# Multiplying the conditioning vector into two weight blocks on TensorE instead of VectorE

## The chip, the cores and the metric

The kernel runs on one core of one Trainium2 chip, one launch for the whole layer. Its engines are named as in the profile: PE is TensorE's matmuls, PEld its weight loads, DVE is VectorE, ACT is ScalarE, POOL is GpSimd, SP is the engine that issues most loads. The metric is the device time of one launch in microseconds, as the median of several runs.

## The reference, cut to what matters

The layer is a decoder block of 1024 tokens and 1024 channels, all in 32-bit floats. A vector `c` conditions it: six vectors of 1024 (shift, scale and gate of two sub-layers) come from one product with a 1024 x 6144 matrix.

```python
c_act = jax.nn.silu(c)
ada = c_act @ ada_w[l] + ada_b[l]
sh1, sc1, gt1, sh2, sc2, gt2 = jnp.split(ada, 6, axis=-1)
h = rmsnorm(x, norm1_g[l]) * (1.0 + sc1) + sh1
z = h @ w_in[l]
q_lat, kv_lat, k_rope, conv_in, gate_logits = jnp.split(z, SPLIT_POINTS, axis=-1)
...
u = glu_a * jax.nn.sigmoid(glu_b)          # the halves of conv_in
u = causal_depthwise_conv(u, conv_w[l], conv_b[l])      # 31 taps, 512 channels
u = jax.nn.silu(layernorm(u, conv_ln_g[l], conv_ln_b[l]))
```

After that come latent attention, the merge of both branches by gates, and a mixture of 32 experts. The change touches the two vectors `sh1` and `sc1` alone, which every column of `h` needs before the first product with `w_in`, and one place in the gates.

## The kernel before, in words

The sums are kept exact by splitting each operand of a large product into a high and a low part (`w_split`, `lo_part`: ACT casts the high part, POOL or DVE subtracts it from the whole). Each product of 128 x 512 is then three PE matmuls.

**The front.** Tokens come in two halves of four tiles, `x0` to `x3` and `x4` to `x7`. A tile is squared with its sum on ACT (`x_square`), its inverse root is found on DVE in Newton steps (`rsqrt_steps`), it is scaled (`x_scales`: tile 6 on ACT, tile 3 on POOL, the others on DVE) and transposed on PE (`x_trans2`, `x_trans`), so that channels lie on partitions: eight blocks `k` of 128 channels for each half. A block is then modulated by its 128 columns of scale and shift (`modulate`), split into high and low (`hi` on ACT, `lo`), and multiplied with the first two pairs of columns of the convolution's input, `wa0`, `wb0`, `wa1`, `wb1` (`prod_h`, `prod_l`, called by `prods`): 12 matmuls for a block and both pairs.

**The modulation.** The first two blocks of `ada_w` (8 MB) are loaded in five steps, for channel blocks 0, 1, (2, 3), (4, 5) and (6, 7). With the matrix's 1024 rows as eight on each partition, `ada_init` and `ada_products` multiply each of the eight slices by its column of `c` and add them up in two accumulators, one DVE instruction for a slice (`ad` times `cact` onto `ac`; the first two slices of steps 3 and 4 are on ACT), and a last instruction adds the two. `ada_sum` sums over partitions on PE, with a column of ones as the moving operand; `modulation` adds the bias. This work is woven between the Newton steps of the next tiles (`weave`, `halves`).

**What sets the order.** In the front the order on PE, ACT, POOL and SP is the order in which the code is written (`manual_schedule`), and the same holds on DVE until the last `u` of the first half, `glu(1, 0, ...)`. After that DVE's order is the scheduler's: the rotary tables, the masks of positions, then the convolution's taps (`conv_taps`, line 757) between the products of `glu` (`u`, line 546). The next blocks of `ada_w` are accumulated between the taps (`ada_block`, line 479).

SP's queue issues the loads in the order in which they are wanted: `x0` to `x3`, step 0 of `ada_w`, the first halves of `wa0` and `wb0`, and so on, up to steps 3 and 4 with `x4` to `x7` behind them. A load waits where its buffer isn't free: two quarters of step 3 take the buffers of `wa0` and `wb0`, and so wait for the subtraction of their second halves on POOL (line 501).

**The convolution's statistics.** The gates are 16 columns `m`, each 48 matmuls on PE (`pg`). After column 5 `conv_stats` transposes the convolution's result on PE (`cT`, line 834) and takes each token's mean and variance on DVE. Its sums are `cacc`, one tile of 128 channels each, four in all; each is done when DVE has put 31 taps on it.

Of the kernel before, what the change touches and what calls it, by code (L numbers as in the profile page):

```python
# [14 lines left out]
F32 = mybir.dt.float32  # L15
# [36 lines left out]
def hybrid_layer(ctx: ExitStack, tc: tile.TileContext, x, c, positions, ada_w, ada_b, norm1_g,  # L52
# [76 lines left out]
    def run(steps):  # L129
        for _ in steps:  # L130
            pass
# [27 lines left out]
    # constants  # L159
# [24 lines left out]
    # vectors that are wanted as columns: one stack of rows, one transpose  # L184
# [27 lines left out]
    # rotary tables, [token, tile, frequency]  # L212
# [65 lines left out]
    cact = consts.tile([P, KD], F32, name="cact")  # L278

    def silu_c():  # L280
        cs_t = pro.tile([P, KD], F32, name="cs_t")
        A.activation(cs_t, c_sb, AF.Tanh, scale=0.5)
        V.scalar_tensor_tensor(cact, cs_t, 1.0, c_sb, op0=OP.add, op1=OP.mult)
        V.tensor_scalar_mul(cact, cact, 0.5)

    # positions: mask of the diagonal blocks, and whether the tiles follow one another
# [61 lines left out]
    XE, SUM, HN = 2, (1, 1, 2), ((2, 2), (0, 2), (0, 2))  # L348
    B0, W0, B1, B2, B3, W4, MB, LO = 4, 2, 2, 2, 6, 2, V, G
    XA, XP = (6,), (3,)  # L350
    ADD, TR, G0, CC0 = 1, (1, 2, 3), 0, 7
# [61 lines left out]
    def ada_init(j, eng):  # L413
        wd = len(STEPS[j]) * P
        g = D // (2 * wd)
        ada_acc[j] = [sa.tile([P, 2, wd], F32, name=f"ac{j}{i}", tag="th" if i else "gt", bufs=2) for i in range(2)]
        for k in range(2):
            a, w, c1 = ada_acc[j][k], adaw_[j][k // g][:, k % g], cact[:, k:k + 1]
            if eng is A:
                A.activation(a.rearrange("p a b -> p (a b)"), w.rearrange("p a b -> p (a b)"), AF.Copy, scale=c1)  # L420
            else:
                V.tensor_scalar(a, w, c1, 0.0, op0=OP.mult, op1=OP.add)
                yield

    def ada_products(j):
        g = D // (2 * len(STEPS[j]) * P)
        acc = ada_acc[j]
        for k in range(2, KD):
            V.scalar_tensor_tensor(acc[k % 2], adaw_[j][k // g][:, k % g], cact[:, k:k + 1], acc[k % 2],
                                   op0=OP.mult, op1=OP.add)  # L430
            yield
        if ADD:
            V.tensor_tensor(acc[0], acc[0], acc[1], op=OP.add)
            yield

    def ada_sum(j):
        ada_ps[j] = ps_o(f"pf{j}")
        m = len(STEPS[j])
        for i in range(2 * m):
            b, jj = divmod(i, m)  # L440
            for h in range(2 - ADD):
                PE.matmul(ada_ps[j][:, i:i + 1], ada_acc[j][h][:, b, jj * P:(jj + 1) * P], ones_c,
                          start=h == 0, stop=h == 1 - ADD)
# [24 lines left out]
    AB, AR, HS, CM = 9, 12, 2, 6  # L468
# [93 lines left out]
    # loads, in the order in which they are wanted  # L562
# [51 lines left out]
    def some(g, n):  # L614
        for _ in range(n):
            next(g, None)
# [14 lines left out]

    run(x_norm(0, 2))
    x23 = x_norm(2, 4)
    some(x23, B0)
    run(ada_init(0, V))
    weave(x23, ada_products(0), W0)
# [3 lines left out]
    column_vectors(0, R_N2)  # L640
    x_trans2(0, 2)
    ada_sum(0)
    run(modulation(0))
    p1 = itertools.chain(ada_init(1, V), ada_products(1))
    some(p1, B1)
    modulate(0, V)
    hi(0, 0)
    x_trans2(2, 2)
    some(p1, 2)
    lo(0, 0, V)  # L650
    prod_h((0,), 0, 0)
    split_part(w1, 0)
    prod_l((0,), 0, 0)
    run(p1)
    p2 = itertools.chain(ada_init(2, V), ada_products(2))
    some(p2, B2)
    x_trans2(4, 2)
    ada_sum(1)
    x_trans2(6, 2)
    run(modulation(1))  # L660
    modulate(1, V)
    hi(0, 1)
    lo(0, 1)
    split_part(w0, 1)
    split_part(w1, 1)
    prods((1,), 0, (0,))
    run(p2)
    run(ada_init(3, A))
    prods((0, 1), 0, (1,), SUM[0], 2)

    def halves(s, later, n0, n1):
        ka, kb = STEPS[s]
        some(later, n0)
        run(modulation(s))
        modulate(ka, V)
        hi(0, ka)
        modulate(kb, MB)
        hi(0, kb)
        some(later, n1)
        lo(0, ka)  # L680
        lo(0, kb, LO)
        run(later)

    halves(2, ada_products(3), *HN[0])
    prods((0, 1), 0, STEPS[2], SUM[1], 3)
    for t in range(4, 4 + XE):
        x_square(t)
    run(ada_init(4, A))
    xe = x_norm(4, 4 + XE)
    some(xe, B3)  # L690
    p4 = weaved(ada_products(4), xe, W4)
    halves(3, p4, *HN[1])
    prods((0, 1), 0, STEPS[3], SUM[2], 4)
    for t in range(4 + XE, NT):
        x_square(t)
    halves(4, x_norm(4 + XE, 8), *HN[2])
# [171 lines left out]
    for m in range(16):  # L868
# [6 lines left out]
        if m == 5:  # L875
            tokn = conv_stats()
# [67 lines left out]
    # q weights with the norm's gain: per head [nope | pe | pe turned], the other way round for odd heads  # L944
# [33 lines left out]
    # tables that the transposed queries are multiplied by  # L978
# [121 lines left out]
    # keys: the first half twice, so that the next pair's can be made ahead  # L1100
# [35 lines left out]
    # tiles of queries, two heads at a time: scores run ahead of the transposed probabilities, these of the values  # L1136
# [78 lines left out]
    # any order of positions: every block of keys, masks from the positions  # L1215
# [66 lines left out]
    # the router's weights with the second norm's scale, its shift as a constant row  # L1282
# [114 lines left out]
    def keep_warm(n_, tag, b_):  # L1397
        # products of no use: without work for some microseconds the tensor engine's clock would be halved
# [35 lines left out]
    # a weight tile takes over the slot of one that is used shortly before it is wanted: gathers go first  # L1434
# [22 lines left out]
    # experts by turns from the groups  # L1457
# [73 lines left out]
    # the order of the products, and after how many more of them each later step of a tile is issued  # L1531
# [53 lines left out]
    # the experts after the first EARLY: sorted by their numbers of rows, those of groups 0, 2 and of 1, 3 by turns;  # L1585
    # place by place fewer rows are provided for
# [129 lines left out]
    # the rows of the last experts are added on chip: to each token its row, by a product with a 0-1 matrix  # L1716
# [18 lines left out]
    for i in range(E + AHEAD[-1]):  # L1735
# [13 lines left out]
        if i == JOIN:  # L1749
            with tc.issue_after(split_[PB]):  # L1750
# [8 lines left out]
                # rows beyond those provided for: counted from 128  # L1759
# [178 lines left out]
```

## Time and profile before

| | |
|---|---|
| median of 3 runs | 1101.34 us (1100.28 to 1103.8) |
| the profiled execution | span 1093.9 us from the first to the last instruction; its time around the span is not listed apart |
| PE busy | 995.7 us, 91% of the span |
| DVE busy | 796.1 us, 73% |
| ACT, POOL busy | 437.3 us, 422.0 us |
| granted TensorE clock, mean | 0.953 |

The shares are means over stages with different limits. In the first 330 us or so DVE is busy almost all the time, and PE stops now and then; later PE is busy without a break for long stretches, and DVE is not. The span is 7.4 us below the median of the runs; a difference within the span is taken as a difference of the time.

### The profile page before, as it was taken

The numbers are of one execution on the slowest core, as the hardware profiler recorded it, in microseconds if no ns is written. First come the engines' busy times: TensorE is split into PE (matmuls) and PEld (weight loads), VectorE is DVE, ScalarE is ACT, GpSimd is POOL, SyncE is SP. The second block draws the span as 40 slices with busy tenths as digits, with TensorE's granted clock in tenths as the row PEclk, the third lists the DMA queues.
The fourth block names the chain that finished last, engine by engine and source line by source line (L and its number), as shares of the span: only waits on it lengthen the run. The fifth ranks groups of instructions, "written<-read, shape, count | busy, mean of one in ns | idle before, by whom it ended". The sixth has DMA issues, their size and how long they took to land. (4 is left out here: it accounts for less than half of the span.)

```text
span 1093.9 us, 16693 instructions
## 1 busy us (share of the span) xinstructions
PE 995.7 (91%) x5744; PEld 841.5 (77%) x5744; DVE 796.1 (73%) x1839; ACT 437.3 (40%) x914; POOL 422.0 (39%) x361
## 2 busy tenths in 40 slices
PE   4697979999599999999999998899998999999991
PEld 2576869988477788778888877678886999997881
DVE  7989999999989815547556665964447888875555
ACT  4453312212123334347666773232223555543343
POOL 5555929823121114114333446630004464454111
PEclk9798989999899999999999999999999999997876
DMA  9902521246574263710000016684656989998813
GB/s 305 307 8 58 140 70 37 92 159 183 172 228 140 105 213 130 249 41 1 1 2 17 6 59 200 212 300 163 258 189 240 314 284 282 301 272 227 269 77 155
DMA packets 97743, 176.79 MB, mean 162 GB/s; under 512 B 14123, under 2 KB 53116, under 8 KB 97648
## 3 DMA queue, kind: packets, MB, share of 16 engines
q1 hardware_dynamic: 82736, 148.33, 40.8%
q0 software_dynamic: 9152, 16.28, 6.3%
q10 hardware_dynamic: 5760, 11.01, 2.8%
q8 instruction: 48, 0.79, 0.3%
q14 instruction: 47, 0.39, 0.1%
HBM read 145.22 MB, written 40.35 MB: 170 GB/s over the span
## 5 line engine op out<-in xcount | busy, mean ns | idle before, releaser
L757 DVE SCALAR_TENSOR_TENSOR cacc<-u,cw,cacc 128x1024 f32<-128x1024 f32 x120 | 173.2, 1496 | 0.0
L1676 PE MATMUL pe<-xT,rg 128*128 128x128 f32 (+7 forms) x512 | 78.9, 288 | 0.1
L1676 PEld LDWEIGHTS pe<-xT,rg 128*128 128x128 f32 x512 | 73.2, 204 | 5.6 <-ACT xT L1671 0.5
L1671 ACT ACTIVATE xT<-xp,h2c 128x128 f32<-128x128 f32 (+7 forms) x128 | 52.4, 434 | 53.4 <-DVE xT L1668 28.8
L1676 PE MATMUL pe<-xT,ru 128*128 128x128 f32 (+7 forms) x512 | 68.8, 293 | 0.0
L1676 PEld LDWEIGHTS pe<-xT,ru 128*128 128x128 f32 x512 | 66.0, 209 | 0.0
L1705 POOL DMA_INDIRECT yscr<-ob,srci x18 | 33.6, 1868 | 59.4 <-DVE ob L1699 30.4
L105 PE MATMUL po<-woh,y 128*128 128x512 f32 x128 | 53.7, 419 | 1.4 <-DVE gm L1331 1.4
L1668 DVE TENSOR_SCALAR xT<-xp,h2c 128x128 f32<-128x128 f32 (+7 forms) x128 | 45.4, 381 | 10.3 <-ACT xT L1671 9.9
L107 PE MATMUL po<-woh,y 128*128 128x512 f32 x128 | 50.4, 394 | 0.0
L106 PE MATMUL po<-wol,y 128*128 128x512 f32 x128 | 50.3, 393 | 0.0
L873 ACT ACTIVATE gt<-pg 128x512 f32<-128x512 f32 x32 | 19.0, 594 | 68.9 <-PE pg L107 68.9
L1518 POOL TENSOR_SCALAR x1n<-x,rst 128x1024 f32<-128x1024 f32 x8 | 9.0, 1121 | 93.9 <-DVE rst L127 82.4
L479 DVE SCALAR_TENSOR_TENSOR acc<-aw,cact,acc 128x1024 f32<-128x1024 f32 x28 | 39.8, 1421 | 3.2 <-DMA aw<-in_ada_w_dram 3.2
L1663 PE MATMUL xp<-ident,xg 128*128 128x128 f32 (+7 forms) x256 | 39.0, 276 | 1.8 <-DMA xg<-xscr,si 1.8
L1655 DVE TENSOR_TENSOR rdl<-rd,rdh 128x1024 fp32r<-128x1024 f32 x30 | 36.7, 1223 | 5.3 <-ACT rdh L1654 5.2
L1654 ACT CAST rdh<-rd 128x1024 fp32r<-128x1024 f32 x30 | 31.4, 1045 | 18.9 <-PE pd L107 17.8
L1081 PE MATMUL mo<-pT,V 128*64 128x128 f32 x576 | 38.5, 278 | 0.0
L1699 DVE SCALAR_TENSOR_TENSOR ob<-pd,wvp,gt2b 128x512 f32<-128x512 f32 (+7 forms) x36 | 26.4, 744 | 16.6 <-DMA yscr<-ob,srci 12.5
L1663 PEld LDWEIGHTS xp<-ident,xg 128*128 128x128 f32 (+7 forms) x256 | 33.5, 194 | 4.0 <-DVE eid L1619 2.6
L1332 POOL TENSOR_TENSOR gm<-gm 128x512 f32<-128x512 f32 x16 | 27.5, 1726 | 22.0 <-DVE gm L1331 19.4
L1081 PEld LDWEIGHTS mo<-pT,V 128*64 128x64 f32 x576 | 30.8, 136 | 5.7 <-issue 5.7
(2071 smaller groups left out, 3141.2 us busy)
## 6 DMA issues: line engine op xcount, KB each, us to landing
aw<-in_ada_w_dram SPq DMA_DIRECT2D x32, 512.0 KB, 3.8
rg<-in_expert_w_gate_dram SPq DMA_DIRECT2D x32, 512.0 KB, 9.6
ru<-in_expert_w_up_dram SPq DMA_DIRECT2D x32, 512.0 KB, 9.2
rd<-in_expert_w_down_dram SPq DMA_DIRECT2D x32, 512.0 KB, 9.3
x<-in_x_dram SPq DMA_DIRECT2D x16, 512.0 KB, 5.5
ad<-in_ada_w_dram SPq DMA_DIRECT2D x32, 256.0 KB, 5.5
wg<-in_w_in_dram SPq DMA_DIRECT2D x16, 512.0 KB, 4.9
gscr<-gt ACTq DMA_DIRECT2D x32, 256.0 KB, 2.9
```

What stands on the lines that cost most here:

```text
L105: PE.matmul(ps, lh, rh, start=first, stop=False)
L106: PE.matmul(ps, lh, rl, start=False, stop=False)
L107: PE.matmul(ps, ll, rh, start=False, stop=last)
L479: V.scalar_tensor_tensor(acc, w, cact[:, k:k + 1], acc, op0=OP.mult, op1=OP.add)
L757: V.scalar_tensor_tensor(a, u[j][:, k:k + T], cw[:, j, k:k + 1], a, op0=OP.mult, op1=OP.add)
L1081: PE.matmul(po[par * DV:(par + 1) * DV, i % 4 * P:(i % 4 + 1) * P], Vt[b][:, 2 * pr + par], pTs[par][:, b * P:(b + 1) * P], start=(b == 0) ...
L1655: V.tensor_tensor(rdl, rd, f32(rdh), op=OP.subtract)
L1663: PE.transpose(p[:, c], xv[:, k, :], ident[:m, :m])
L1668: split_.append(V.tensor_scalar(xT[:, ks], p[:, c], h2c[:, 0, k:k + 1], h2c[:, 1, k:k + 1], op0=OP.mult, op1=OP.add).ins)
L1671: A.activation(xT[:, ks], p[:, c], AF.Identity, scale=h2c[:, 0, k:k + 1], bias=h2c[:, 1, k:k + 1])
L1676: PE.matmul(pa[:, o:o + m], w[:, k * P:(k + 1) * P], xT[:, k * P:k * P + m], start=(k == 0), stop=(k == KD - 1))
L1705: s_ = G.indirect_dma_start(out=yscr, out_offset=bass.IndirectOffsetOnAxis(ap=src[:m], axis=0), in_=ob[:m], in_offset=None, bounds_check=T ...
```

## The change

The eight products of a step are done on PE now (`ada_mm`). `silu_c` writes `c` 32 times side by side (`crep`), so that a slice's column of `c` is a stationary operand of 128 rows and 32 columns, and the slice of `ada_w` is the moving operand, 256 or 512 columns wide. Slices 0 to 3 go to four different groups of 32 partitions of one PSUM bank, slices 4 to 7 are added to them. ACT copies the bank to `ac`, and `ada_sum` sums over the four groups with a column that is one at partitions 0, 32, 64 and 96 (`sel4`). Nothing of a step is left on DVE but `modulation` and `modulate`; the low parts of the first half's blocks are all subtracted on DVE now, of which seven were on POOL. The Newton steps of the tiles are no longer woven with anything, and those of tiles 6 and 7, with their squares, stand behind step 4's split. `conv_stats` is called after gate column 6, `conv_act` and the later blocks of `ada_w` one or two columns later.

```diff
     cact = consts.tile([P, KD], F32, name="cact")
+    crep_ = []
+    sel4 = pro.tile([P, 1], F32, name="sel4")
 
     def silu_c():
         cs_t = pro.tile([P, KD], F32, name="cs_t")
         A.activation(cs_t, c_sb, AF.Tanh, scale=0.5)
         V.scalar_tensor_tensor(cact, cs_t, 1.0, c_sb, op0=OP.add, op1=OP.mult)
         V.tensor_scalar_mul(cact, cact, 0.5)
...
+        crep = sa.tile([P, KD, 32], F32, name="crep", tag="gt", bufs=2)
+        crep_.append(crep)
+        V.tensor_copy(crep, cact[:, :, None].to_broadcast([P, KD, 32]))
+
+        si = pro.tile([P, 1], I32, name="sel4i")
+        V.tensor_single_scalar(si, pidx_i, 31, op=OP.bitwise_and)
+        V.tensor_scalar(sel4, si, 0.0, None, op0=OP.is_equal)
...
-    XE, SUM, HN = 2, (1, 1, 2), ((2, 2), (0, 2), (0, 2))
-    B0, W0, B1, B2, B3, W4, MB, LO = 4, 2, 2, 2, 6, 2, V, G
+    XE, SUM = 2, (1, 2, 4)
     XA, XP = (6,), (3,)
-    ADD, TR, G0, CC0 = 1, (1, 2, 3), 0, 7
+    TR, G0, CC0 = (1, 2, 3), 0, 7
...
-    def ada_init(j, eng):
+    def ada_mm(j):
+
         wd = len(STEPS[j]) * P
         g = D // (2 * wd)
-        ada_acc[j] = [sa.tile([P, 2, wd], F32, name=f"ac{j}{i}", tag="th" if i else "gt", bufs=2) for i in range(2)]
-        for k in range(2):
-            a, w, c1 = ada_acc[j][k], adaw_[j][k // g][:, k % g], cact[:, k:k + 1]
-            if eng is A:
-                A.activation(a.rearrange("p a b -> p (a b)"), w.rearrange("p a b -> p (a b)"), AF.Copy, scale=c1)
-            else:
-                V.tensor_scalar(a, w, c1, 0.0, op0=OP.mult, op1=OP.add)
-                yield
-
-    def ada_products(j):
-        g = D // (2 * len(STEPS[j]) * P)
-        acc = ada_acc[j]
-        for k in range(2, KD):
-            V.scalar_tensor_tensor(acc[k % 2], adaw_[j][k // g][:, k % g], cact[:, k:k + 1], acc[k % 2],
-                                   op0=OP.mult, op1=OP.add)
-            yield
-        if ADD:
-            V.tensor_tensor(acc[0], acc[0], acc[1], op=OP.add)
-            yield
+        p = ps_o(f"am{j}")
+        for k in range(KD):
+            q = 32 * (k % 4)
+            PE.matmul(p[q:q + 32, :2 * wd], crep_[0][:, k], adaw_[j][k // g][:, k % g].rearrange("p b n -> p (b n)"),
+                      start=k < 4, stop=k >= 4)
+        ada_acc[j] = sa.tile([P, 2, wd], F32, name=f"ac{j}", tag="th", bufs=2)
+        A.copy(ada_acc[j].rearrange("p b n -> p (b n)"), p[:, :2 * wd])
 
     def ada_sum(j):
         ada_ps[j] = ps_o(f"pf{j}")
         m = len(STEPS[j])
         for i in range(2 * m):
             b, jj = divmod(i, m)
-            for h in range(2 - ADD):
-                PE.matmul(ada_ps[j][:, i:i + 1], ada_acc[j][h][:, b, jj * P:(jj + 1) * P], ones_c,
-                          start=h == 0, stop=h == 1 - ADD)
+            PE.matmul(ada_ps[j][:, i:i + 1], ada_acc[j][:, b, jj * P:(jj + 1) * P], sel4, start=True, stop=True)
 
...
-    AB, AR, HS, CM = 9, 12, 2, 6
+    AB, AR, HS, CM = 10, 14, 2, 8
...
+    def step(j, eng):
+        run(modulation(j))
+        for k in STEPS[j]:
+            modulate(k, V)
+        for k in STEPS[j]:
+            hi(0, k)
+            lo(0, k, eng)
+
     run(x_norm(0, 2))
-    x23 = x_norm(2, 4)
-    some(x23, B0)
-    run(ada_init(0, V))
-    weave(x23, ada_products(0), W0)
+    run(x_norm(2, 4))
     for k in range(0, KD, 2):
         x_trans2(k, 0)
     split_part(w0, 0)
     column_vectors(0, R_N2)
+    ada_mm(0)
     x_trans2(0, 2)
+    x_trans2(2, 2)
     ada_sum(0)
-    run(modulation(0))
-    p1 = itertools.chain(ada_init(1, V), ada_products(1))
-    some(p1, B1)
-    modulate(0, V)
-    hi(0, 0)
-    x_trans2(2, 2)
-    some(p1, 2)
-    lo(0, 0, V)
+    step(0, V)
+    x_trans2(4, 2)
+    ada_mm(1)
+    x_trans2(6, 2)
+    split_part(w1, 0)
     prod_h((0,), 0, 0)
-    split_part(w1, 0)
+    ada_sum(1)
+    step(1, V)
     prod_l((0,), 0, 0)
-    run(p1)
-    p2 = itertools.chain(ada_init(2, V), ada_products(2))
-    some(p2, B2)
-    x_trans2(4, 2)
-    ada_sum(1)
-    x_trans2(6, 2)
-    run(modulation(1))
-    modulate(1, V)
-    hi(0, 1)
-    lo(0, 1)
+    prods((1,), 0, (0,))
     split_part(w0, 1)
     split_part(w1, 1)
-    prods((1,), 0, (0,))
-    run(p2)
-    run(ada_init(3, A))
+    ada_mm(2)
     prods((0, 1), 0, (1,), SUM[0], 2)
-
-    def halves(s, later, n0, n1):
-        ka, kb = STEPS[s]
-        some(later, n0)
-        run(modulation(s))
-        modulate(ka, V)
-        hi(0, ka)
-        modulate(kb, MB)
-        hi(0, kb)
-        some(later, n1)
-        lo(0, ka)
-        lo(0, kb, LO)
-        run(later)
-
-    halves(2, ada_products(3), *HN[0])
-    prods((0, 1), 0, STEPS[2], SUM[1], 3)
+    step(2, V)
+    ada_mm(3)
     for t in range(4, 4 + XE):
         x_square(t)
-    run(ada_init(4, A))
-    xe = x_norm(4, 4 + XE)
-    some(xe, B3)
-    p4 = weaved(ada_products(4), xe, W4)
-    halves(3, p4, *HN[1])
+    prods((0, 1), 0, STEPS[2], SUM[1], 3)
+    step(3, V)
+    run(x_norm(4, 4 + XE))
+    ada_mm(4)
     prods((0, 1), 0, STEPS[3], SUM[2], 4)
+    step(4, V)
     for t in range(4 + XE, NT):
         x_square(t)
-    halves(4, x_norm(4 + XE, 8), *HN[2])
+    run(x_norm(4 + XE, 8))
...
-        if m == 5:
+        if m == 6:
             tokn = conv_stats()
         if m in (CM, CM + 1):
             conv_act(m - CM, tokn)
```

On PE, at the end of the front, `am` is the bank that the new products write, `ad` the loaded slices, `pf` the sum over partitions, and `pa`, `pb` the products of the first half. In the changed kernel the stretch around step 4's products reads:

```order
L598 MATMUL pa_262<-hT0l,wa1h 128x512
L598 MATMUL pb_263<-hT0l,wb1h 128x512
L428 MATMUL am_561<-ad_231,crep 32x512 x2
L428 MATMUL am_561<-ad_232,crep 32x512 x2
L428 MATMUL am_561<-ad_233,crep 32x512 x2
L428 MATMUL am_561<-ad_234,crep 32x512 x2
L592 MATMUL pa_260<-hT0h,wa0h 128x512
L593 MATMUL pa_260<-hT0h,wa0l 128x512
```

All 24 products of channel blocks 4 and 5 now stand between these eight and the sum `pf` of step 4; before, 12 of them stood ahead of that sum and 12 behind it.

On ACT, in the same place, `hT0h` is a block's high part, the line with `ms` is a square with its sum, and `th` is the `tanh` of the first `glu`. Before:

```order
L627 CAST hT0h<-xn_346 128x512
L360 ACTIVATE hT1l,ms<-x_242 128x1024
L360 ACTIVATE hT1l,ms<-x_244 128x1024
L627 CAST hT0h<-xn_353 128x512
L627 CAST hT0h<-xn_355 128x512
L367 ACTIVATE x_242<-x_242,rstd 128x1024
L545 ACTIVATE th_681<-pb_255 128x512
```

And now:

```order
L622 CAST hT0h<-xn_341 128x512
L431 COPY ac_570<-am_561 128x512
L622 CAST hT0h<-xn_348 128x512
L622 CAST hT0h<-xn_350 128x512
L368 ACTIVATE hT1l,ms<-x_243 128x1024
L368 ACTIVATE hT1l,ms<-x_245 128x1024
L375 ACTIVATE x_243<-x_243,rstd 128x1024
L540 ACTIVATE th_687<-pb_261 128x512
```

The squares of tiles 6 and 7 moved from ahead of the last two blocks' high parts to behind them, next to the scaling of tile 6 that needs their result.

On PE, at the statistics, `pg` is a gate product and the four tiles `cacc` are told apart by their numbers. Before:

```order
L834 MATMUL cT_2302<-ident,cacc_1189 128x128
L834 MATMUL cT_2302<-ident,cacc_1221 128x128
L834 MATMUL cT_2310<-ident,cacc_1189 128x128
L834 MATMUL cT_2310<-ident,cacc_1221 128x128
L105 MATMUL pg_2452<-hT0h,wg6h 128x512
L106 MATMUL pg_2452<-hT0l,wg6h 128x512
L107 MATMUL pg_2452<-hT0h,wg6l 128x512
L834 MATMUL cT_2302<-ident,cacc_1253 128x128
L834 MATMUL cT_2310<-ident,cacc_1253 128x128
```

And now:

```order
L107 MATMUL pg_2334<-hT1h,wg6l 128x512
L809 MATMUL cT_2370<-ident,cacc_1195 128x128
L809 MATMUL cT_2370<-ident,cacc_1227 128x128
L809 MATMUL cT_2370<-ident,cacc_1259 128x128
L809 MATMUL cT_2378<-ident,cacc_1195 128x128
L809 MATMUL cT_2378<-ident,cacc_1227 128x128
L809 MATMUL cT_2378<-ident,cacc_1259 128x128
L105 MATMUL pg_2520<-hT0h,wg7h 128x512
```

Before, 288 gate products stand ahead of the first piece and 76 more between it and the transposes of the fourth tile (after the 3 that are shown, 367 in all). Now 336 stand ahead of it and 31 behind, again 367 in all; the rest of the transposes follows at the same places among the gate products as before.

## Rows read from the trace of the kernel before

**Rows 1.** Waits of PE, first 420 us: waited for; us, times, longest

```profile
PE pb L105 <- DVE u L546: 12.2, 2, 6.5
PE pf L442 <- DVE ac L433: 12.0, 4, 6.9
PE cT L834 <- DVE cacc L757: 11.6, 1, 11.6
```

**Rows 2.** Busy time by stretch: engines, granted clock, share and rate of the DMAs

```profile
30.00:35.00 5.00, 1.88 (x8) 1.16 (x7) 5.00 (x4) 3.01 (x6) 5.00 (x4) 1.00 0.35 111
35.00:57.00 22.00, 16.51 (x56) 12.56 (x56) 21.15 (x43) 7.69 (x14) 9.49 (x6) 0.69 0.99 326
...
71.00:311.00 240.00, 215.57 (x1055) 186.33 (x1054) 239.72 (x254) 58.54 (x107) 124.89 (x77) 0.95 0.38 111
311.00:395.00 84.00, 79.29 (x373) 63.98 (x372) 64.83 (x130) 26.37 (x43) 14.35 (x6) 1.00 0.48 153
```

**Rows 3.** Costliest groups of DVE in the first 66 us: busy us, mean ns

```profile
L429 DVE SCALAR_TENSOR_TENSOR ac<-ad,cact,ac 128x512 f32<-128x512 f32 (+1 forms) x30 | 29.7, 1039 | 0.0
...
L433 DVE TENSOR_TENSOR ac<-ac,ac 128x512 f32<-128x512 f32 (+1 forms) x5 | 3.9, 771 | 0.1
```

**Rows 4.** Timeline of DVE: start us, us, line, operation [idle before]

```profile
7.27 0.15 DVE L110 TENSOR_SCALAR ms<-ms 128x1 f32<-128x1 f32 x1 [1.39 <-ACT hT1l L360]
...
8.89 0.28 DVE L127 SCALAR_TENSOR_TENSOR rstd<-nwt,rstd 128x1 f32<-128x1 f32 x2
...
70.65 0.69 DVE L546 SCALAR_TENSOR_TENSOR u<-th,pa 128x512 f32<-128x512 f32 x1 [4.29 <-ACT th L545]
```

**Rows 5.** The tile `ad` (steps of `ada_w`): issues of its loads, time to landing

```profile
L409 SPq DMA_DIRECT2D ad<-in_ada_w_dram x32: 367/468/1153, 3.1 to 41.9; - x32
...
DMA to landing us min/median/max: 2.7/5.5/7.7
```

**Rows 6.** Waits of SP's queue, 24 to 48 us

```profile
SPq L409 <- POOL wa0l L501: 5.7, 1, 5.7
```

**Rows 7.** Timeline of POOL at the second half of `wa0`

```profile
29.77 1.70 POOL L501 TENSOR_TENSOR hT0l<-xn,hT0h 128x512 fp32r<-128x512 f32 x1 [3.18 <-ACT hT0h L627]
31.41 1.72 POOL L501 TENSOR_TENSOR wa0l<-wa,wa0h 128x512 fp32r<-128x512 f32 x1
```

**Rows 8.** Timeline of PE in the attention: products on two column blocks

```profile
561.87 1.97 PE L1081 MATMUL mo<-pT,V 128*64 128x128 f32 x32
563.77 0.50 PE L105 MATMUL u31S<-kb11h,qh 128*128 128x512 f32 x1
```

**Rows 9.** Line 1402: products of 128 x 512 in 32-bit floats, ns min/median/max, starts

```profile
L1402 PE MATMUL warmtr<-gt2b,ident x8: 592/592/648, 837.0 to 840.0; 128*128 128x512 f32 x8
```

**Rows 10.** Timeline of PE: step 4's sum over partitions

```profile
57.48 1.02 PE L442 MATMUL pf<-ones_c,ac 128*128 128x1 f32 x8 [0.73 <-DVE ac L433]
```

**Rows 11.** Timeline of ACT at the end of the front

```profile
50.78 1.05 ACT L360 ACTIVATE hT1l<-x 128x1024 fp32r<-128x1024 f32 x1
...
52.77 0.19 ACT L360 ACTIVATION_READ_ACCUMULATOR hT1l<-x 128x1 f32 x1
59.60 1.14 ACT L627 CAST hT0h<-xn 128x512 fp32r<-128x512 f32 x2 [6.64 <-DVE xn L461]
63.94 1.15 ACT L367 ACTIVATE x<-x,rstd 128x1024 f32<-128x1024 f32 x1 [3.20 <-DVE rstd L127]
```

**Rows 12.** Timeline of PE around the convolution's transposes

```profile
291.93 0.69 PE L834 MATMUL cT<-ident,cacc 128*128 128x128 f32 x2 [11.63 <-DVE cacc L757]
...
292.85 0.63 PE L106 MATMUL pg<-hT0l,wg6h 128*128 128x512 f32 x1
293.27 0.63 PE L107 MATMUL pg<-hT0h,wg6l 128*128 128x512 f32 x1
...
299.48 0.39 PE L106 MATMUL pg<-hT1l,wg6h 128*128 128x512 f32 x1
299.71 0.39 PE L107 MATMUL pg<-hT1h,wg6l 128*128 128x512 f32 x1
...
311.05 0.38 PE L834 MATMUL cT<-ident,cacc 128*128 128x128 f32 x2
```

**Rows 13.** Timeline of DVE: the last tap

```profile
308.89 1.27 DVE L757 SCALAR_TENSOR_TENSOR cacc<-u,cw,cacc 128x1024 f32<-128x1024 f32 x1
```

## The prediction, made before the changed kernel was run

> **What bounds the kernel now.** I read the waits of PE first, because PE is the busiest engine: in the first 420 us it waits on DVE three times for long, on the products `u` of the first half and of its followers (12.2 us), on the accumulators `ac` of the modulation (12.0 us) and on the convolution's sums `cacc` (11.6 us) [rows 1]. Then the busy time by stretch, to see what DVE does meanwhile: from 71 to 311 us it is busy 239.72 of 240 us, while PE is busy 215.57, and from 311 to 395 us PE is busy 79.29 of 84 [rows 2]. So there are three stages. Up to 71 us a front that ends when DVE makes the last `u` of the first half, at 70.65 [rows 4]. Then 240 us of DVE without a gap, which end with the last tap at 308.89 + 1.27 = 310.16 [rows 13]; PE needs that tap for the transposes of the fourth `cacc`, at 311.05 [rows 12]. From there on PE is the bound. The rows of a stage's own bound decide what an edit in it is worth: DVE work that goes from the front shortens the launch only by as much as the 70.65 comes earlier.
>
> **What leaves DVE.** The accumulations of line 429 cost it 29.7 us and the closing sums of line 433 3.9 us [rows 3], together 33.6 of the first 66 us. The rotary tables and the masks can't take the place, since they are issued behind the last `u` of the front. So this time turns into idle time, and the front is set by what was late next: the loads, and a chain of PE, ACT and DVE behind them. What DVE gets in return (the copies of `c`, the column `sel4`, seven subtractions of 128 x 512) costs nothing, since it falls in that idle time; before, DVE would have had to carry it on the path.
>
> **When step 4 has landed.** Its last load is issued at 41.9, and a load of `ada_w` lands after 5.5 us [rows 5]: 47.4. On the way SP waited 5.7 us for POOL's subtraction on `wa0` [rows 6], which began at 31.41, right behind a subtraction of 1.70 us on the first half's block 1 [rows 7]. That one leaves POOL, and the cast in front of it comes earlier, as block 1 no longer waits for the chain on DVE. The DMAs paid for this wait with a share of 0.35 in the five microseconds from 30 to 35, against 0.99 in the 22 behind [rows 2]: (0.99 - 0.35) / 0.99 x 5 = 3.2 us lost. Bounds are 0 (something else holds the buffer) and 5.7 (the whole wait). I take 3.2, since the DMAs can't give back more than they lost: step 4 has landed at 44.2. PE is ready by then: between step 3's products and step 4's stand 24 products and a sum, 8.4 us by the prices below, while the 3.1 MB of `x4`, `x5` and step 4 take 9.6 us at 326 GB/s [rows 2].
>
> **The new products.** No row shows a matmul on four column blocks. A 32-bit product of 128 x 512 is two records, and eight of them start over 3.0 us, 0.43 us apart [rows 9]. The attention has products on two column blocks: 32 records of 128 columns from 561.87 to 563.77, 59 ns each [rows 8], where a quarter of 0.43 would be 107. So two blocks overlap to 1.8 of 2. A step of 512 columns has 8 products, 16 records: 6.9 us if no block overlaps another (twice that at the lower clock), 3.8 if they do by pairs, 1.7 if all four do perfectly. I carry the 0.9 of the attention over to four blocks: 16 x 0.43 / 3.6 = 1.9 us. Below 1.7 nothing is possible, as the columns have to pass.
>
> The Trainium skill, in "TensorE: Matmul & The Clock Gate", section "Part 3: Packing small matmuls — row/col tiling", says that outputs on different column groups run at the same time, and gives 2.38 times for three groups. That is 0.79 a group where the attention's rows show 0.9 for two; an estimate by it is 2.2 us for a wide step and 0.6 us more for the two steps that count here, which would make the time 1097.5. No run here shows four groups, so the sum stays with the rows.
>
> **From there to the last `u`.** Step by step, with the order that is now written: step 4's products 1.9. Then all 24 products of blocks 4 and 5, one pass of 0.23 each, as from 299.48 to 299.71 [rows 12], 5.5. Then the sum over partitions, `modulation`, `modulate` and two high parts: before, from 57.48 [rows 10] to 59.60 + 1.14 = 60.74 [rows 11], 3.3. The squares of tiles 6 and 7 stand behind that on ACT now: 50.78 to 52.96, 2.2 [rows 11]. The Newton steps, undisturbed by POOL as at the start, 7.27 to 9.17, 1.9 [rows 4]. The scaling of tile 6, 1.15 [rows 11]. From its end to the last `u` it was 70.65 - 65.09 = 5.6 [rows 4, 11], with the same instructions. 44.2 + 1.9 + 5.5 + 3.3 + 2.2 + 1.9 + 1.2 + 5.6 = 65.8, against 70.65: **4.9 us earlier**. Of the 33.6 us freed, then, a seventh shows. The new late thing is ACT's queue: squares that were done 6.6 us before the high parts [rows 11] now stand on the path with the Newton steps and the scaling, 5.3 us together.
>
> **The 240 us of DVE** keep their instructions and their order, so the last tap comes 4.9 us earlier too.
>
> **The statistics one gate column later.** The number of gate products ahead of the fourth tile's transposes is 367 before and after, so the move doesn't give PE more work to do before it needs the last tap. Before, PE waited 11.6 us for the third tile [rows 1, 12] and came 311.05 - 310.16 = 0.9 us after the last tap. Now 48 products (11.0 us) fill the first wait, and after the third tile PE has only 31 left: 291.93 + 0.35 + 31 x 0.23 = 299.4, and it waits 10.8 us for the last tap. That saves the 0.9. But behind an idle time of this length PE started at the lower clock, 0.42 us a product, as from 292.85 to 293.27 [rows 12], for about seven products, 7 x 0.19 = 1.4 us, which were hidden ahead of the last tap and now stand behind it. Net 0.5 us lost. The later calls of `conv_act` and of `ada_w`'s last blocks meet the 4.7 us of waits that PE has up to 395 us; I count them at nothing, with 2 us to either side.
>
> **Sum:** 4.9 - 0.5 = 4.4 us off the span of 1093.9, so 1089.5. The median of the runs lies 7.4 above that span, and with the same distance the time is 1101.34 - 4.4 = **1096.9 us**.
>
> **Rivals.** *The overlap or the clock is worse.* If column blocks overlap only by pairs, steps 3 and 4 cost 1.9 more each and the time is 1100.7. If PE runs the end of the front at the lower clock, 24 products cost 24 x 0.19 = 4.6 more and it is 1101.5. For it: the clock was 0.69 from 35 to 57 us [rows 2]. Against it: that clock followed idle times of PE which waited for `ac`, and these go. Together about 1101, no change. *Blocks don't overlap at all* (the other side): 6.9 us for each wide step, 5.0 more than counted, and three of them one behind the other on PE make 15 us: 1112. From 4.1 us a step on, steps 3 and 4 alone, with 2.2 more each, eat the gain of 4.4. For it, nothing in this trace with four blocks; against it, the two blocks of the attention [rows 8]. *The gate column really fills the wait:* if the last tap came earlier than 4.9 us, say because the 240 us of DVE shrink with less of POOL beside them, PE's 10.8 us before the fourth tile would go and the time would be 1086. For it, PE is idle there as long as a column lasts; against it, 239.72 of 240 busy, and the order.
>
> **Chances.** My forecast 0.56 (with 1093 to 1101 as its own range: 44.2 may be 42 to 47, and the end may move by 2), pairs or clock 0.22, no overlap 0.12, the filled wait 0.10. A measurement of this kernel tells a change from none at about 0.3%, 3.3 us. Faster than that: 0.7 of the forecast, all of the filled wait and a little of the second case, 0.51. Within it: 0.28 of the forecast and 0.7 of the second case, 0.31. Slower: the rest, 0.18. A range that leaves out no more than 2 in 10 goes from 1087, which cuts off the filled wait, to 1108, between the second case and the third.
>
> **What would show it.** Right: the last `u` of the first half near 65.8; `am` of a wide step in about 2 us; DVE idle some 30 us before that; SP without the wait for POOL, or with 2 us of it; ACT's squares of tiles 6 and 7 directly behind two high parts, and PE waiting for the transposes of the second half; DVE full for 240 us after; PE waiting some 11 us before the fourth `cacc`, not the third. Wrong: `am` above 4 us; the last `u` after 70; a stretch of DVE with gaps between there and the last tap; or PE passing the transposes without a wait.

## The result, and the profile after

The changed kernel takes **1090.15 us** in the median of its first six runs (1081.65 to 1092.42), against 1102.47 for the six runs of the kernel before beside them: ratio 0.9887, with a 95% interval of 0.9848 to 0.9926. The forecast was 1096.9, so the direction is right and the gain of 12.3 us is nearly three times the 4.4 that the sum had. Two further measurements of the same kernel gave 0.9964 (0.9934 to 0.9993) and 0.9937 (0.9906 to 0.9967). The ratios leave out a few executions in a slower state. Weighted by their intervals, the three make 0.9936 ± 0.0037, some 7 us with 4 us to either side; but the first two lie outside each other's intervals, so the true uncertainty is larger. What of this is the change, and what is not, took most of the experiments.

The profiled execution has a span of 1083.4 us. First the front, in which the forecast placed the whole gain. The waits of PE in the first 420 us; the columns are us in total, times, longest:

```profile
PE cT L809 <- DVE cacc L732: 11.8, 2, 10.5
PE pb L105 <- DVE u L541: 11.7, 2, 6.6
...
PE pa L592 <- ACT hT0h L622: 1.7, 1, 1.7
PE pf L438 <- ACT ac L431: 1.5, 1, 1.5
PE xT L389 <- ACT x L375: 1.4, 1, 1.4
```

The 12.0 us in which PE waited for `ac` [rows 1] are down to 1.5, and two small waits are new: for step 4's high parts, and for the tile scaled on ACT. The stretches in between, to be laid beside [rows 2]:

```profile
30.00:35.00 5.00, 3.46 (x17) 2.24 (x15) 1.36 (x4) 1.99 (x4) 4.41 (x4) 0.87 1.08 342
35.00:57.00 22.00, 20.20 (x102) 12.96 (x102) 10.09 (x36) 7.31 (x13) 0.46 (x4) 0.95 0.94 303
...
67.00:307.00 240.00, 215.16 (x1058) 186.09 (x1057) 239.63 (x254) 58.89 (x107) 125.03 (x77) 0.96 0.38 112
```

The third busy time is DVE's: 10.09 of 22 us where it was 21.15, and again without a gap for the 240 us after the front. PE's granted clock from 35 to 57 us is 0.95 instead of 0.69, and the DMAs have filled the hole at 30 to 35 (a share of 1.08 instead of 0.35). Now the ends of the stages. The timeline of DVE, with the last `u` of the first half and the last tap [rows 4, 13]:

```profile
62.33 0.69 DVE L541 SCALAR_TENSOR_TENSOR u<-th,pa 128x512 f32<-128x512 f32 x1 [1.10 <-ACT th L540]
67.00 0.69 DVE L541 SCALAR_TENSOR_TENSOR u<-th,pa 128x512 f32<-128x512 f32 x1 [3.98 <-ACT th L540]
...
305.46 1.27 DVE L732 SCALAR_TENSOR_TENSOR cacc<-u,cw,cacc 128x1024 f32<-128x1024 f32 x1
```

And the timeline of PE at the convolution's transposes [rows 12]:

```profile
288.51 0.66 PE L809 MATMUL cT<-ident,cacc 128*128 128x128 f32 x4 [1.29 <-DVE cacc L732]
...
306.78 0.69 PE L809 MATMUL cT<-ident,cacc 128*128 128x128 f32 x2 [10.54 <-DVE cacc L732]
307.12 0.78 PE L106 MATMUL pg<-hT1l,wg7h 128*128 128x512 f32 x1
307.70 0.63 PE L107 MATMUL pg<-hT1h,wg7l 128*128 128x512 f32 x1
```

The front is 70.65 - 67.00 = 3.65 us shorter, the fourth tile's transposes come 311.05 - 306.78 = 4.3 us earlier, and the wait of PE stands in front of the fourth tile instead of the third. Up to here the trace goes the way that the forecast said, with other sizes: it had 4.9 us for the front and, with the 0.9 us saved behind the last tap, 5.8 at the fourth tile. The 10.5 us between the two spans are not all here, though. After 311 us the code of both kernels is the same but for the columns at which `conv_act` and the last blocks of `ada_w` stand, and yet one stretch differs by as much again. Here is the window from the router's last product to the last product of the experts, first of the kernel before, then of the changed one; the columns are those of [rows 2]:

```profile
830.90:1054.48 223.58, 218.85 (x1504) 197.43 (x1504) 158.10 (x378) 102.52 (x231) 97.67 (x66) 0.91 0.84 260
```

```profile
825.50:1043.94 218.44, 211.89 (x1505) 190.51 (x1505) 157.84 (x378) 101.30 (x230) 99.76 (x66) 0.95 0.86 266
```

The same 1504 product records (1505 in the second window) take 223.58 us at a mean granted clock of 0.91 and 218.44 at 0.95. So 5.4 us were won up to the router's end (830.9 to 825.5) and 5.1 us in the experts.

### The profile page after: what moved, and what is told of

The parts are those of the page before. It is cut to its first block, busy times and chain, and to the rows that moved or that the text cites. A ratio compares the mean times of both kernels' runs of the same rounds, so it can differ in the third digit from the quotient of the medians.

```text
span 1083.4 us, 16818 instructions
## 1 busy us (share of the span) xinstructions
PE 992.9 (92%) x5824; PEld 832.9 (77%) x5824; DVE 765.0 (71%) x1808; ACT 436.7 (40%) x915; POOL 409.6 (38%) x354
## 5 line engine op out<-in xcount | busy, mean ns | idle before, releaser
L732 DVE SCALAR_TENSOR_TENSOR cacc<-u,cw,cacc 128x1024 f32<-128x1024 f32 x120 | 171.0, 1476 | 0.0
L1651 PEld LDWEIGHTS pe<-xT,rg 128*128 128x128 f32 x512 | 71.0, 198 | 6.6 <-DVE xT L1643 1.1
L1651 PE MATMUL pe<-xT,ru 128*128 128x128 f32 (+7 forms) x512 | 66.1, 285 | 0.0
L1651 PEld LDWEIGHTS pe<-xT,ru 128*128 128x128 f32 x512 | 63.3, 201 | 0.0
L1680 POOL DMA_INDIRECT yscr<-ob,srci x18 | 35.8, 1987 | 57.9 <-DVE ob L1674 20.2
```

The costliest lines, as they stand in the source:

```text
L732: V.scalar_tensor_tensor(a, u[j][:, k:k + T], cw[:, j, k:k + 1], a, op0=OP.mult, op1=OP.add)
L1651: PE.matmul(pa[:, o:o + m], w[:, k * P:(k + 1) * P], xT[:, k * P:k * P + m], start=(k == 0), stop=(k == KD - 1))
L1680: s_ = G.indirect_dma_start(out=yscr, out_offset=bass.IndirectOffsetOnAxis(ap=src[:m], axis=0), in_=ob[:m], in_offset=None, bounds_check=T ...
```

## The experiments

Every ratio is to the kernel before, in runs on the same chip as the kernel tried.

**1. The kernel before, once more** (no edit).

> The kernel before, unchanged, to see how its runs spread and what the granted clock has to do with it. Theory (the front gained 3.7 us, the rest of the measured difference is TensorE's clock in the last experts, which differs from run to run and is not tied to the change): ratio to the kernel before 0.997 to 1.003, spans that spread by about 10 us, and span minus span x (1 - clock) nearly the same in all runs (1041 to 1047 us). Its profile shows a last u of the first half at 70.7, and between 990 and 1055 us another sum of low-clock time than the 18.8 us of the first profile, by several us. Rival (the changed kernel's later phases always meet a better clock): every run has a clock of 0.956 or less, and 17 to 20 us are lost between 990 and 1055 again.

Ratio 1.0003 (0.9961 to 1.0045), 1098.11 us in the median, and twelve runs from 1090.19 to 1108.37. The profiled execution has a span of 1088.6, 5.3 us less than the first. The front ends at 70.94 and the router at 831.8, later than in the first profile; the gain is in the experts alone. The same window of this run:

```profile
831.80:1049.16 217.36, 210.41 (x1505) 189.91 (x1504) 157.52 (x378) 102.13 (x231) 100.14 (x66) 0.95 0.88 268
```

217.36 us at 0.95 against 223.58 at 0.91, with not one instruction changed. That is as much as the changed kernel gained there. The theory's other claim, that span minus the clock's loss, span x (1 - clock), is nearly one number for all runs, fell: in these twelve runs it goes from 1031.8 to 1047.2. Over the 35 runs of before that stand beside experiments 1 to 4, one more us of that loss goes with only about 0.5 us more of span. A reason could be that PE also waits at the lower clock where nothing depends on it; that is not shown.

**2. The changed kernel with the statistics back at column 5.**

```diff
-    AB, AR, HS, CM = 10, 14, 2, 8
+    AB, AR, HS, CM = 9, 12, 2, 6
-        if m == 6:
+        if m == 5:
             tokn = conv_stats()
```

> The changed kernel with the statistics back behind gate column 5 (and conv_act, the last blocks of ada_w and their end at the columns of before). Theory (the move of the statistics is worth nothing): within 3 us of the changed kernel, ratio to before 0.986 to 0.992; last u of the first half at 67.0, PE's wait of about 11 us back at the third tile's transposes. Rival (the move gives the 6 us that the forecast lacks): ratio 0.994 to 0.998, that is 1095 to 1100 us.

0.9945 (0.9906 to 0.9984). PE's wait is back at the third tile (9.91 us, at 287.22) and the fourth tile's transposes are at 306.13, where the changed kernel has them at 306.78. The router ends at 828.7, where three profiles of the changed kernel have 825.5, 827.2 and 827.6. So the move may be worth 1 to 3 us. The ratio fell into the range of the rival; but the second and third measurement of the changed kernel (experiment 6) lie to either side of it, so it shows no difference.

**3. The kernel before with the statistics at column 6** (the reverse edit).

> The kernel before with the statistics moved by one gate column and nothing else. Theory (the move is worth nothing): ratio 0.997 to 1.003; PE waits some 11 us before the fourth tile's transposes and not the third's, the transposes of the fourth begin 0 to 1 us later than 311.0. Rival (the move is worth 6 to 8 us): ratio 0.993 to 0.995.

0.9989 (0.9947 to 1.0032): alone, the move can't be told from nothing. PE's wait stands in front of the fourth tile here too, as expected. Its transposes begin at 314.92, later than the expected 311 to 312; the profiled execution is one of the longest of its kernel (span 1106.3), and nothing is concluded from that.

**4. All eight products on one column block.**

```diff
-            q = 32 * (k % 4)
-            PE.matmul(p[q:q + 32, :2 * wd], ...
-                      start=k < 4, stop=k >= 4)
+            PE.matmul(p[:32, :2 * wd], ...
+                      start=k == 0, stop=k == KD - 1)
```

> The changed kernel with the eight products of a step all on the first column block, one behind the other (16 records of 512 columns at 0.43 us, 6.9 us for a wide step), the sum then taken over 32 partitions. Theory (the overlap of the four blocks carries the front's gain): am of steps 3 and 4 takes 6.9 us each, step 4's products start 2 us later and end 7 us later than in the changed kernel, the last u of the first half comes at 73 to 75 instead of 67.0, and the time is 6 to 8 us above the changed kernel's: ratio to before 0.992 to 0.997. Rival (the loads set the front, the overlap is hidden): last u at 67 to 69 and ratio 0.986 to 0.990. Rival of the forecast (no overlap costs 15 us): ratio 1.002 to 1.009.

1.0064 (1.0028 to 1.0100), slower than the kernel before. Timeline of PE, the last two steps here, and then the last in the changed kernel:

```profile
40.04 7.05 PE L427 MATMUL am<-ad,crep 128*32 128x512 f32 x16
53.93 7.05 PE L427 MATMUL am<-ad,crep 128*32 128x512 f32 x16
```

```profile
45.72 2.04 PE L428 MATMUL am<-ad,crep 128*32 128x512 f32 x16
```

7.05 / 2.04 = 3.46: four blocks overlap to 0.86 of perfect, or slightly better, since the 2.04 us hold a short wait for the last slices' load (see below). The last `u` came at 80.41, 13.4 us later. My expectation for this run had 73 to 75, because I let the loads hide the first two wide steps; they hid little, 1.6 of three times 5.0 us, and the forecast's own rival (15 us, 1112) was nearer to the 1106.21 us of the median.

**5. The eight products on two column blocks** (`q = 32 * (k % 2)`, `start=k < 2`, `stop=k >= KD - 2`, sum over 64 partitions).

> The changed kernel with the eight products of a step on two column blocks instead of four. Theory (the overlap is 0.86 to 0.9 of the number of blocks, as 7.05 us against 2.04 showed for four): a wide step at the full clock takes 3.8 to 4.1 us; each of the three wide steps ends about 2 us later than with four blocks, the last u of the first half at 71 to 73 us, ratio to before 0.996 to 1.003, which is the forecast's rival of no change. Rival (two blocks overlap fully, 3.5 us or less, or the loads cover it): last u at 67 to 70, ratio as in the changed kernel.

```profile
47.40 3.63 PE L428 MATMUL am<-ad,crep 128*32 128x512 f32 x16
```

7.05 / 3.63 = 1.94 for two blocks. Last `u` at 71.73, 4.7 us later than with four, ratio 0.9969 (0.9934 to 1.0003). Of the rival that the forecast gave 0.22, the half with the pairs would have come true had the blocks overlapped only so: the front is as long as before, and no gain is shown.

**6. The changed kernel a second and a third time.**

> The changed kernel, unchanged, beside the three below. Theory (of the gain, some 4 us are the front and what follows from it, and the larger ratio of the first six runs was partly the luck of the clock in the last experts): ratio to the kernel before 0.990 to 0.996, spans that spread by 10 us, front and fourth cacc as in its first profile (67.0 and 306.8 within 1 us), low-clock time behind 985 us another than the 17.9 us of the first profile. Rival (the whole change is worth 1.1%): ratio 0.986 to 0.990 again.

> The changed kernel a third time, since its first two measurements (ratios 0.9887 and 0.9964) lie outside each other's intervals. Theory (the change is worth 4 to 6 us, which is seen up to the end of the output projection in every profile, and the rest is the clock in the last experts): ratio 0.991 to 0.998; last po product at 821 to 824 us. Rival (1.1% is the true size and the second measurement was the odd one): ratio 0.986 to 0.991.

0.9964 (0.9934 to 0.9993) and 0.9937 (0.9906 to 0.9967). The fronts agree with the first profile (last `u` at 66.78 and 66.85). The fourth tile's transposes are at 304.14 and 304.20, 2.6 us earlier than in the first profile, which the expectation had not; the router ends at 827.2 and 827.6, 2 us later. The experts' window of the second run:

```profile
827.20:1052.47 225.27, 220.88 (x1504) 198.77 (x1504) 157.39 (x378) 101.46 (x230) 98.89 (x66) 0.90 0.84 258
```

6.8 us more than in the first profile of the same kernel, at a clock of 0.90. In the third it is 225.58 at 0.90. Both lie above the 217.36 of the unchanged kernel of experiment 1. Over eleven profiles of these kernels this window goes from 217.4 us at 0.95 to 228.0 at 0.89, and the two of the kernel before (223.58 and 217.36) lie within the range of the changed kernel and its variants or below it. The theory held for the ratios; its places were off at the fourth tile.

**7. Squares, Newton steps and scaling of tiles 6 and 7 ahead of step 4's products.**

```diff
     ada_mm(4)
+    for t in range(4 + XE, NT):
+        x_square(t)
+    run(x_norm(4 + XE, 8))
     prods((0, 1), 0, STEPS[3], SUM[2], 4)
     step(4, V)
-    for t in range(4 + XE, NT):
-        x_square(t)
-    run(x_norm(4 + XE, 8))
```

> The changed kernel with the squares, Newton steps and scaling of tiles 6 and 7 issued ahead of the products and the sum of step 4 instead of behind them. Theory (they stand on the path, but PE waits only 1.36 us for them, since it has products of step 4 meanwhile): PE's wait for the scaled tile goes, the last u of the first half comes 1.2 to 2 us earlier (65.0 to 65.8), and the time stays within 2 us of the changed kernel's. Rival (all 5.3 us of squares, Newton steps and scaling are on the path, as the forecast had them): last u at 61 to 63, ratio 0.005 below that of the changed kernel.

The last `u` came at 66.47, only 0.5 us earlier than 67.00, less than expected; the ratio is 0.9911 (0.9879 to 0.9943) where the changed kernel beside it had 0.9964.

> The kernel with the squares moved ahead once more. Theory (its stages differ from the changed kernel's by 0.3 us, so its 5 us in the medians were the last experts' clock): ratio within 0.003 of the third run of the changed kernel beside it. Rival (the order is worth 0.5%): ratio 0.004 to 0.006 below it again.

Last `u` at 67.18, 0.9942 (0.9906 to 0.9977) beside 0.9937: as fast as the changed kernel, no faster. The 0.5% of the first measurement didn't return; the experts' window of that first one was 228.0 us, so its profile doesn't explain it either.

**8. Rotary tables' DVE work behind step 2.**

```diff
     step(2, V)
+    angles = rotary()
...
     with tc.issue_after(last_dve[0]):
-        angles = rotary()
         masks()
```

> The changed kernel with the rotary tables' DVE work issued behind step 2, into DVE's idle time of the front, instead of behind the last u. Theory (from the last u to the last tap DVE is the bound, so that work taken out of this stretch is worth its full time, up to the end of the second half's products at 86 us): the last u of the first half at 67 to 68, the first u of the second half at 86 to 89 instead of 96.1, PE's wait of 6.6 us there gone, the last tap at 294 to 299 instead of 306.7, and the time 8 to 12 us below the changed kernel's. Rival (PE's waits move elsewhere, or the last experts' clock takes it back): within 4 us of the changed kernel.

0.9920 (0.9873 to 0.9968), which can't be told from the 0.9964 (0.9934 to 0.9993) of the changed kernel beside it; the 8 to 12 us expected are not seen. With the edit of experiment 7 on top:

> Both of the above: squares of tiles 6 and 7 ahead of step 4's products, rotary tables behind step 2. Theory: the two add up, last u of the first half at 65.0 to 66.5, last tap at 292 to 298, the time 9 to 13 us below the changed kernel's, ratio to before 0.978 to 0.985. Rival (rotary on DVE behind step 2 delays the chain of steps 3 and 4, and the front gets longer): last u at 68 to 71, the rest as in the run with the rotary tables alone.

0.9953 (0.9924 to 0.9981). In the latter's trace the first `u` of the second half comes at 88.46 instead of 96.14, 7.7 us earlier, but the last tap is at 304.63, where the profiles of the changed kernel have 302.81 to 305.46. Windows from about this `u` to the one behind the next ten taps, first of this run, then of the changed kernel; busy times of PE, PEld, DVE, ACT, POOL:

```profile
88.40:121.10 32.70, 30.41 (x135) 24.84 (x133) 32.46 (x15) 11.16 (x15) 32.70 (x13) 1.00 0.50 133
```

```profile
96.70:121.60 24.90, 24.64 (x98) 20.23 (x99) 24.90 (x20) 9.01 (x13) 18.68 (x8) 0.89 0.34 96
```

The taps came earlier and fell beside POOL's subtractions, which fill this window without a gap (32.70 of 32.70). DVE's timeline shows what that does to them, here and in the changed kernel:

```profile
91.02 6.66 DVE L732 SCALAR_TENSOR_TENSOR cacc<-u,cw,cacc 128x1024 f32<-128x1024 f32 x2
```

```profile
97.86 1.28 DVE L732 SCALAR_TENSOR_TENSOR cacc<-u,cw,cacc 128x1024 f32<-128x1024 f32 x1
```

3.3 us for a tap beside these subtractions, 1.28 without them. By 121 us the 7.7 us are 0.5. The tables also delayed the front (last `u` at 68.74). The theory that DVE work taken out of the full stretch is worth its time fell. The Trainium skill, "GPSIMD Engine Reference", section "8. Key points", says that GpSimd shares its SBUF interfaces with VectorE and contends with its instructions that have two SBUF inputs. A tap is one, and 3.3 against 1.28 us agrees.

## Why the prediction was right, and where it was off

**Bound and place: right; the size partly by luck.** The front ends with the same `u`, and DVE is full after it (239.63 of 240). The gain up to the fourth tile is 4.3 us in the first profile and 6.9 in the other two (311.05 to 304.14 and 304.20), where the forecast had 4.9 + 0.9 = 5.8. The stretch from the last `u` to the last tap, which was to keep its length, took 238.2 us before, 238.5 in the first profile after, and 236.0 in the other two; why the same instructions took 2.4 us less there is open. The ends of the router, 830.9 and 831.8 before, 825.5, 827.2 and 827.6 after, differ by 4.6 in the mean. That is the measured size of the change where the clock of the experts has no part in it, and it lies within the 7 ± 4 us of the three ratios. It is a rough number, since from the fourth tile to the router's end the three profiles after took 518.7, 523.1 and 523.4 us, and those before 519.9 and 520.5. That it is so near to the 4.4 of the sum is partly luck, since the front gave less than counted and the stages behind it vary by more than the difference.

**The step that was off: "step 4 has landed at 44.2".** The last load of step 4 landed 5.9 us after its issue at 40.65, at 46.6. Before, it landed at 47.3. So the loads gained 0.7 us and not the 3.2 that the sum had for the wait of SP. Here are the first load of step 3 and the last of step 4, each with its time to landing, and then the first 30 us of the program by the columns of [rows 2]; first before:

```profile
24.78 1.05 SPq L409 DMA_DIRECT2D ad<-in_ada_w_dram  x1
DMA to landing us min/median/max: 5.5/5.5/5.5
...
41.88 0.37 SPq L409 DMA_DIRECT2D ad<-in_ada_w_dram  x1
DMA to landing us min/median/max: 5.4/5.4/5.4
...
0.00:30.00 30.00, 13.80 (x54) 10.13 (x55) 23.03 (x78) 14.68 (x33) 15.70 (x40) 1.00 1.04 307
```

And after:

```profile
26.49 1.17 SPq L417 DMA_DIRECT2D ad<-in_ada_w_dram  x1
DMA to landing us min/median/max: 6.3/6.3/6.3
...
40.65 0.37 SPq L417 DMA_DIRECT2D ad<-in_ada_w_dram  x1
DMA to landing us min/median/max: 5.9/5.9/5.9
...
0.00:30.00 30.00, 17.67 (x106) 10.29 (x107) 13.61 (x60) 16.19 (x36) 15.21 (x40) 1.00 1.03 286
```

The hole did close (0.35 to 1.08, SP's wait 5.7 to 1.5): from the first of these landings to the second it is 13.8 us instead of 17.0, which is the 3.2 of the sum. But step 3's first load landed at 32.8 instead of 30.3, 2.5 us later, since the same loads in the same order came at 286 GB/s instead of 307 in the first 30 us. Why they were slower is open; the forecast let everything ahead of the hole keep its time.

"PE is ready by then" fell with it at 44.2, but costs little. PE had waited for step 3's loads too, between the products of step 3:

```profile
36.61 0.37 PEld L428 LDWEIGHTS am<-ad,crep 128*32 128x32 f32 x4 [1.32 <-DMA ad<-in_ada_w_dram]
38.09 0.17 PEld L428 LDWEIGHTS am<-ad,crep 128*32 128x32 f32 x4 [1.12 <-DMA ad<-in_ada_w_dram]
...
46.60 0.25 PEld L428 LDWEIGHTS am<-ad,crep 128*32 128x32 f32 x6 [0.31 <-issue]
```

and then had its 24 products and the sum to do, 39.11 to 45.72. It began step 4's products at 45.72, 0.9 us ahead of the last landing, and the last slices' weights went in at 46.60, right behind it. The products of a slice are two records 0.43 us apart, so those of the last slices could not have ended before about 47.5 (an estimate), against 47.69, had PE been ready earlier. The sum had the end of these products at 44.2 + 1.9 = 46.1, so this step was 1.6 us late; the front gained 3.65 and not 4.9.

**The rest of the chain: right, to 0.4 us in each term.** Step 4's products 1.97 (45.72 to 47.69; forecast 1.9), 24 products 5.6 (5.5), sum to high parts 3.1 (3.3), squares 2.2 (2.2), Newton steps 1.9 (1.9), scaling 1.15 (1.15), to the last `u` 5.2 (5.6). ACT's and PE's timelines give these:

```profile
53.28 0.94 PE L438 MATMUL pf<-sel,ac 128*128 128x1 f32 x8
...
61.87 0.44 PE L389 MATMUL xT<-ident,x 128*128 128x128 f32 x2 [1.36 <-ACT x L375]
```

```profile
55.23 1.14 ACT L622 CAST hT0h<-xn 128x512 fp32r<-128x512 f32 x2 [6.79 <-DVE xn L456]
56.28 1.06 ACT L368 ACTIVATE hT1l<-x 128x1024 fp32r<-128x1024 f32 x1
...
60.67 1.15 ACT L375 ACTIVATE x<-x,rstd 128x1024 f32<-128x1024 f32 x1 [2.20 <-DVE rstd L127]
```

But "5.3 us together" on the path overstates what they cost. PE's wait behind them is 1.36 us, since products of step 4 run meanwhile, and experiment 7 got back only 0.5 us or nothing.

**The overlap: right.** 0.9 of two blocks was carried over to four; it measured 1.94 of 2 and 3.46 of 4. The Trainium skill's page "TensorE: Matmul & The Clock Gate", section "Part 3: Packing small matmuls — row/col tiling", gives 2.38 for three, 0.79 a group. Here it is 0.97 and 0.86 a group, so the measurement decides for the rows. The other half of that rival, the lower clock at the end of the front, did not come: with the waits for `ac` gone, the clock was 0.95.

**The statistics.** The wait of 10.8 us before the fourth tile was 10.54, and seven products ran at the lower clock behind it, 0.43 us apart, as forecast. PE came right behind the last tap (305.46 + 1.27 = 306.73, then 306.78), so the 0.9 us were saved. The net loss of 0.5 was not seen; experiment 2 allows a gain of 1 to 3 us, experiment 3 shows none. The rival in which the gate column fills the wait is out: its condition, a shorter stretch of DVE, came in two of three profiles, but only by 2.4 us, and PE still waits 9.4 to 10.5 us there.

**"Nothing later": right for the change, wrong for the runs.** The forecast took the other runs to lie at a fixed distance from the profiled one. The experts' window moved by up to 10.6 us from profile to profile (217.4 to 228.0), and six runs of each kernel were too few to average that out. One thing stays open. The first six runs and the next twelve of the changed kernel differ by more than their intervals allow, and I can't say whether the chip that they ran on has a part in it.

## What to carry to other kernels

Before a difference of medians is explained, profile the unchanged kernel a second time and compare stage by stage: a stage that differs as much between two runs of one program can't be put down to an edit. Time freed on an engine is worth what the next late thing leaves of it, here a ninth (3.65 of 33.6 us), and a near tie between a load and an engine (PE free at 45.72, the last load at 46.6) should be carried with both outcomes. A hole in the loads that closes brings the loads behind it forward by its length only if those ahead of it keep their times, so read the landing itself (3.2 us expected here, 0.7 measured). Work moved earlier can land beside another engine that slows it, so ask what runs there before counting the time as won.

## What the runs showed of the hardware

- TensorE's granted clock in the experts is not the same from run to run. In the second profile of the changed kernel the window from 985 to 1045 us had PE busy for 59.38 of 60 us at a mean clock of 0.66, in the first 55.86 of 60 at 0.83; in both the clock goes back and forth between 2.4 and 1.2 GHz, and not every fall has an idle time of PE in front of it. What decides it is not settled.
- A tap of 128 x 1024 on DVE takes 1.28 us alone and up to 3.4 us beside POOL's subtractions; the 120 taps of the changed kernel have a median of 1.272 us and a mean of 1.476. The 15 that take 2.1 to 3.4 us all lie beside subtractions of 128 x 672 or 128 x 1024. 40 others lie beside POOL's products and sums of 128 x 16 for the rotary part and keep their 1.27 us; there most of POOL's small instructions take 1.23 us by the profile, about a tap's length, so it seems to be POOL that waits.
- Products of 128 x 512 in 32-bit floats on 32 columns each overlap to 1.94 on two column blocks (7.05 against 3.63 us) and to 3.46 on four (7.05 against 2.04).
